# A hybrid decoder layer on one Trainium2 core: the order of small matmuls in attention and retention

## The chip, the cores and the metric

One NeuronCore of one Trainium2 chip runs the whole step. Its engines work side by side and wait for each other through semaphores: TensorE (PE in the profile; its weight loads are PEld), VectorE (DVE), ScalarE (ACT), GpSimd (POOL) and SyncE (SP), which here issues most DMAs. The metric is the device time of one execution in microseconds; the time before is the median of three runs.

## The reference, cut to what matters

One layer on 512 prompt tokens and 8 sequences of 4 sample tokens, all in float32: a combined projection, then eight heads of retention beside sixteen heads of sliding-window attention, an output projection, and a convolutional FFN. The two parts that the change touches are these:

```python
def retention_chunk(S, qkv):              # 4 chunks of 128 tokens; 8 heads, q and k 64 wide, v 128 wide
    q, k, v = qkv
    ...
    scores = jnp.einsum('bihd,bjhd->bhij', q, k) * dmask[None]
    o = jnp.einsum('bhij,bjhv->bihv', scores, v)
    o = o + jnp.einsum('bihd,bhdv->bihv', q, S) * jnp.exp((idx + 1.0)[:, None] * lg[None, :])[None, :, :, None]
    ...
def sink_attention(q, kk, vv, qpos, kpos, sinks):   # 16 query heads, 2 key heads, 64 wide; window of 128
    s = jnp.einsum('bnqkgd,bnskd->bnkgqs', q.astype(F32), kk.astype(F32)) * (SWA_DH ** -0.5)
    ...
    p = p / (jnp.sum(p, axis=-1, keepdims=True) + jnp.exp(sink - m))
    return jnp.einsum('bnkgqs,bnskd->bnqkgd', p, vv.astype(F32))
```

## The kernel before, in words

Most matmuls are float32 products made of three products of rounded halves (`mm3`: lines 174 and 178, 96 matmuls of 128x272 for one projection of 128 columns). Thirty-four such projections fill the first 604 us: per pair of retention heads one of q, one of k and two of v, then the attention's k and v, its eight q pairs and the eight gates. The output projection follows (to about 798 us), then the FFN, which takes the rest.

Retention and attention are cut into Python generators that are advanced between the projections' matmuls: `project` calls `slot_fast` after 32 and 64 of its 96 matmuls and `slot` after 48, and both again at its end. The generator `retention` is in the list `active` (advanced by `slot`), `swa_stream` and after it `swa_sample` in the list `fast`. So the small matmuls stand in PE's queue between those of the projections. The framework that records the program moves some instructions on each engine a little; PE then works its queue in order.

A head is 64 wide, and two heads share the 128 partitions: `half(0)` is partitions 0 to 63 and `half(1)` is 64 to 127. A product over one head therefore runs over 64 rows of PE's array (the profile writes 64\*128: 64 rows, 128 columns), where a projection runs over all 128 (128\*128). Four places mix the two kinds:

- `scores(i)` in `swa_stream`, 16 blocks of work (two heads of each key head, 128 queries each): for each key head `kv` and each `j`, a matmul over 128 rows with `kX[kv]` (line 721, the two cross products of the halves of q and k) and then one over 64 rows with `kH` (line 722) into the same place of the PSUM tile `sc`. VectorE then masks, scales and takes the maximum (line 725); `softmax` follows, and `turn` transposes the result on PE (line 700) for `outputs` (line 683).
- `scores(hh)` in `retention`, once for each half and each of four head pairs: four matmuls over 64 rows (line 494). Half 0 is issued one slot before half 1. Each float32 matmul of this kind is two passes in the profile, so 4 matmuls are 8 records.
- The outputs of a chunk in `retention` (lines 529 and 531): for each half, scores times v over 128 rows, then q times the state S over 64 rows. Chunk 0 has no state, so there are three chunks with both kinds for each of four head pairs: 12 places.
- The end of `swa_sample` (lines 809 and 810): for each of two key heads and eight sequences, a matmul over 128 rows that yields 64 output rows (128\*64) and one over 32 rows (32\*64).

PSUM is used through `small()`: a ring of four tiles with one name, each a bank of 128x512 float32.

Of the kernel before, what the change touches and what calls it, by code (L numbers as in the profile page):

```python
# [106 lines left out]
def trunk_kernel(  # L107
# [9 lines left out]
    pe, dve, act, pool = nc.tensor, nc.vector, nc.scalar, nc.gpsimd  # L117
# [3 lines left out]
    mult, add, sub = ALU.mult, ALU.add, ALU.subtract  # L121
# [77 lines left out]
    def small():  # L199
        return ps.tile([128, 512], F32, name="sm", tag="sm")  # L200
# [4 lines left out]
    def b4(shape, name, dtype=F32):  # L205
        return at.tile(shape, dtype, name=name, tag="b4", bufs=4)

    def g2(shape, name, dtype=F32):
        return at.tile(shape, dtype, name=name, tag="g2", bufs=4)

    def toks(c):
        return slice(128 * (c % 2), 128 * (c % 2) + 128)

    def half(i):
        return slice(64 * i, 64 * i + 64)

    def flat(a):
        return a.rearrange("p a b -> p (a b)")

    def halves_of(a):  # L220
        return a.rearrange("p (u c) -> p u c", u=2)
# [125 lines left out]
    band = late[:, 1128:1384]  # L347
# [21 lines left out]
    dmt = rtab[:, 0:1024].rearrange("p (h i) -> p h i", h=RH)  # L369
# [112 lines left out]
    def retention(p, q3, k2, v2):  # L482
# [5 lines left out]
            pool.tensor_copy(out=dst, in_=qd[half(hh), :, 256:272].rearrange("p u (b t) -> p u b t", t=4))  # L488
        sms = []

        def scores(hh):
            pss = small()
            for c in range(4):
                pe.matmul(pss[:, 128 * c:128 * c + 128], lhsT=kr[half(hh), c // 2, toks(c)], rhs=qr[half(hh), c // 2, toks(c)], start=True, stop=True)
            sm = g2([128, 4, 128], "smk")
            dve.tensor_tensor(out=sm, in0=pss.rearrange("p (c i) -> p c i", c=4),
                              in1=dmt[:, 2 * p + hh, :].unsqueeze(1).broadcast_to([128, 4, 128]), op=mult)
            sms.append(sm)

        yield  # L500
        pt, pts = to_tokens(kr, ksm)
# [1 line left out]
                          in1=kdt[:, 2 * p:2 * p + 2].unsqueeze(1).unsqueeze(3).broadcast_to([128, 4, 2, 64]), op=mult)  # L503
        for hh in range(2):
            dve.tensor_scalar(out=kd2[32 * hh:32 * hh + 32, half(hh)], in0=pts[:, half(hh)],
                              scalar1=kdst[:32, 2 * p + hh:2 * p + hh + 1], scalar2=None, op0=mult)
        scores(0)
        yield
        scores(1)
        for hh in range(2):  # L510
            pss = small()
            pe.matmul(pss[:32, 0:32], lhsT=ksm[half(hh), :], rhs=qsm[half(hh), :], start=True, stop=True)
            r = slice(32 * hh, 32 * hh + 32)
            dve.tensor_tensor(out=sm2[r, r], in0=pss[:32, 0:32], in1=dmst[:, 2 * p + hh, :], op=mult)
        S, ons, on = None, None, None
# [9 lines left out]
        for c in range(4):  # L525
            yield
            obs = [small(), small()]
            for hh in range(2):
                pe.matmul(obs[hh][:, 0:128], lhsT=sms[hh][:, c, :], rhs=vt[:, hh, c, :], start=True, stop=(S is None))
                if S is not None:  # L530
                    pe.matmul(obs[hh][:, 0:128], lhsT=qd[half(hh), c // 2, toks(c)], rhs=S[half(hh), :], start=False, stop=True)
            up = small()
            for hh in range(2):
                pe.matmul(up[half(hh), 0:128], lhsT=kd[:, c, half(hh)], rhs=vt[:, hh, c, :], start=True, stop=True)
            Sn = at.tile([128, 128], F32, name="S", tag="S", bufs=3)
            if S is None:
                dve.tensor_copy(out=Sn, in_=up[:, 0:128])
            else:
                dve.scalar_tensor_tensor(out=Sn, in0=S, scalar=gt[:, p:p + 1], in1=up[:, 0:128], op0=mult, op1=add)
            S = Sn  # L540
            if c == 0:
                ob = small()
                for b in range(NB):
                    pe.matmul(ob[:64, 0:128], lhsT=qm[:, 64 * b:64 * b + 64], rhs=Ss[:, b, :], start=(b == 0), stop=False)
                pe.matmul(ob[:64, 0:128], lhsT=sm2, rhs=v2, start=False, stop=True)
            if c == 1:
                pt = small()
                pe.transpose(out=pt[:, 0:64], in_=ons, identity=ident[:64, :64])
                for hh in range(2):
                    act.activation(out=C[:, 2 * p + hh, :, 256:272], in_=halves_of(pt[:, 32 * hh:32 * hh + 32]), func=AF.Copy,  # L550
                                   scale=gnw[:, 2 * p + hh:2 * p + hh + 1])
                for g in range(2):
                    up = small()
                    pe.matmul(up, lhsT=kd2, rhs=vm[:, 4 * g:4 * g + 4, :].rearrange("p b v -> p (b v)"), start=True, stop=True)
                    sl = Ss[:, 4 * g:4 * g + 4, :]
                    dve.scalar_tensor_tensor(out=sl, in0=sl, scalar=gt[:, 4 + p:5 + p], in1=up.rearrange("p (b v) -> p b v", b=4), op0=mult, op1=add)
                st(out=ret_s[0, :, 2 * p:2 * p + 2].rearrange("b h d v -> (h d) b v"), in_=Ss)
            if c == 2:
                back(on, 0)
            if c % 2 == 0:  # L560
                on = g2([128, 2, 2, 128], "on")
            norm_rows([o[:, 0:128] for o in obs], [on[:, c % 2, hh, :] for hh in range(2)])
            if c == 0:
                ons = at.tile([64, 128], F32, name="ons", tag="ons", bufs=1)
                norm_rows([ob[:64, 0:128]], [ons])
                vm = b4([64, NB, 128], "vm")
                dve.tensor_tensor(out=vm, in0=v2.unsqueeze(1).broadcast_to([64, NB, 128]), in1=bmask[:64, :].unsqueeze(2).broadcast_to([64, NB, 128]), op=mult)
# [5 lines left out]
    kH = at.tile([128, SEQ], F32R, name="kH")  # L573
    kX = [at.tile([128, SEQ], F32R, name=f"kX{i}") for i in range(2)]
    vS = at.tile([128, 4, 2, 128], F32R, name="vS")
    vsk = at.tile([32, 128], F32, name="vsk")
# [47 lines left out]
    scl, qSs = {}, {}  # L624
# [47 lines left out]
    def swa_stream():  # L672
# [34 lines left out]
        def scores(i):  # L707
            hp, n = i // 4, i % 4
            h0 = 2 * hp
            qS = qSs[hp, n // 2]  # L710
            k0 = max(0, 128 * (n - 1))
            w, off = (128, 128) if n == 0 else (256, 0)
            s = b4([128, 4, 256], "s")
            mx = at.tile([128, 4], F32, name="mx", tag="mx", bufs=3)
            den = at.tile([128, 4], F32, name="den", tag="den", bufs=3)
            for kv in range(2):
                sc = small()
                for j in range(2):
                    q_ = qS[:, j, kv, toks(n)]
                    o = sc[:, 256 * j:256 * j + 256]  # L720
                    pe.matmul(o, lhsT=q_, rhs=kX[kv][:, k0:k0 + 256], start=True, stop=False)  # L721
                    pe.matmul(o, lhsT=q_[half(kv)], rhs=kH[half(kv), k0:k0 + 256], start=False, stop=True)  # L722
                for j in range(2):
                    i_ = 2 * j + kv
                    dve.tensor_tensor_reduce(out=s[:, i_, 0:w], in0=sc[:, 256 * j:256 * j + w], in1=band[:, off:off + w], scale=scl[h0 + j][:, n, kv:kv + 1],
                                             scalar=-3.0e38, op0=add, op1=ALU.max, accum_out=mx[:, i_:i_ + 1])
            softmax(s, w, mx, flat(sinkb[:, h0:h0 + 2, :]), flat(nsinkb[:, h0:h0 + 2, :]), den)
            probs[i] = s, w
            if n == 0:
                split_q(hp, 1)  # L730
# [14 lines left out]
    def swa_sample():  # L745
        kc, vc = b4([128, NB, 128], "kc"), b4([128, NB, 128], "vc")
# [17 lines left out]
        for u in range(2):  # L764
            dve.tensor_tensor(out=qsa[:, 4 * u:4 * u + 4].rearrange("p b h t -> p h b t"),
                              in0=C[:, 8:16, u, 256:272].rearrange("p h (b t) -> p h b t", t=4),
                              in1=y[:, :, 16 * u:16 * u + 16].rearrange("p h (b t) -> p h b t", t=4), op=mult)
# [11 lines left out]
        for kv in range(2):  # L779
            r = half(kv)  # L780
            sc = small()
            scv = sc[:, 0:320].rearrange("p (g j) -> p g j", g=2)
            for b in range(NB):
                q_ = qsa[r, b, :, :].rearrange("p h t -> p (h t)")
                o = slice(32 * (b % 4), 32 * (b % 4) + 32)
                pe.matmul(scv[o, b // 4, 0:128], lhsT=q_, rhs=kcT[r, b, :], start=True, stop=True, tile_position=(64 * kv, 32 * (b % 4)))
                pe.matmul(scv[o, b // 4, 128:160], lhsT=q_, rhs=ksmp[r, :], start=True, stop=True, tile_position=(64 * kv, 32 * (b % 4)))
            for g in range(2):
                i = 2 * kv + g
# [9 lines left out]
        pTs = b4([128, 2, 512], "pTs")  # L799
# [2 lines left out]
        yield  # L802
        po = small()
        pov = po[:, 0:256].rearrange("p (b x) -> p b x", b=NB)
        for kv in range(2):
            r = half(kv)
            for b in range(NB):
                o = 128 * (2 * kv + b // 4) + 32 * (b % 4)
                pe.matmul(pov[r, b, :], lhsT=vc[:, b, r], rhs=pTs[:, 0, o:o + 32], start=True, stop=False)
                pe.matmul(pov[r, b, :], lhsT=vsk[:, r], rhs=pTs[:32, 1, o:o + 32], start=False, stop=True)  # L810
        for u in range(2):
            dve.tensor_copy(out=C[:, 8:16, u, 256:272].rearrange("p h (b t) -> p h b t", t=4),
                            in_=pov[:, 4 * u:4 * u + 4, :].rearrange("p b (h t) -> p h b t", t=4))
# [515 lines left out]
```

## Time and profile before

| What | Value |
| --- | --- |
| Runs | 2279.88, 2281.12, 2283.51 us; median 2281.12 |
| Profiled execution | 2281.43 us, span 2279.7 us |
| PE busy | 2215.3 us, 97% of the span, 17159 matmuls |
| DVE, ACT, POOL busy | 1632.7 us (72%), 1010.3 us (44%), 292.7 us (13%) |
| Chain that ended last | PE 66%, issue 17%, DVE 8%, DMA 5% |
| Mean granted clock of TensorE | 0.984 |

The span runs from the first to the last instruction; the execution's own time lies 1.7 us above it. Busy time counts overlapping records once, so a PE that is 97% busy may still hold small matmuls that run one by one. The chain is followed back from the last instruction, at each step to what released it.

### The profile page before, as it was taken

What the parts mean: (1) busy time and instruction counts of PE and PEld (TensorE: products, weight loads), DVE (VectorE), ACT (ScalarE), POOL (GpSimd) and SP (SyncE); (2) the same over time, 40 slices, a digit from 0 to 9 for tenths busy, and PEclk for the clock granted to TensorE, in tenths of its full rate; (3) what the DMA queues carried; (4) which work ended last, traced back from release to release, by engine and by line L of the source; (5) the groups of instructions that cost most, each with busy time, mean ns of one, the idle gap of its engine ahead of it and who ended that gap; (6) DMA issues with size and microseconds to landing.
All of it is one profiled execution on the core that took longest, in us unless ns stands there. A gap on an engine that the chain in (4) does not pass through costs nothing.

```text
span 2279.7 us, 42004 instructions
## 1 busy us (share of the span) xinstructions
PE 2215.3 (97%) x17159; PEld 2161.7 (95%) x17159; DVE 1632.7 (72%) x2457; ACT 1010.3 (44%) x1612; POOL 292.7 (13%) x463
## 2 busy tenths in 40 slices
PE   8999999999999979999999999999998999899998
PEld 7999999999999979999999999999998999898898
DVE  5545466766435788888888888888888766767775
ACT  5122234556413454444444444444446444445443
POOL 1000000000001312212112112112112101101000
PEclk8999999999999989999999999999999999999999
DMA  9333333213373343443444344344347556657553
GB/s 284 99 95 89 82 83 79 73 54 104 78 162 117 101 136 110 126 132 119 125 123 123 116 128 121 117 128 126 118 123 228 140 121 178 155 135 212 145 147 97
DMA packets 452656, 286.52 MB, mean 126 GB/s; under 512 B 46320, under 2 KB 430640, under 8 KB 452080
## 3 DMA queue, kind: packets, MB, share of 16 engines
q1 hardware_dynamic: 433376, 222.16, 35.7%
q0 software_dynamic: 19088, 61.68, 9.0%
q8 instruction: 134, 2.20, 0.4%
q14 instruction: 58, 0.48, 0.1%
HBM read 231.38 MB, written 47.67 MB: 122 GB/s over the span
## 4 chain that ended last, share of the span: by engine, by line
PE 66%; issue 17%; DVE 8%; DMA 5%; POOL 2%; ACT 1%; SPq 1%; DVEq 0%; POOLq 0%; ACTq 0%
PE acc L174 18%; PE acc L178 9%; PE bx L1090 6%; PE bx L1089 6%; PE bx L1092 6%; PE zy L1090 5%; PE zy L1089 5%; PE zy L1092 4%; DMA uraw<-in_w_up_dram 3%; DVE ulo L151 3%; POOL x_keep L1257 1%; DMA A_lo<-hx_keep 1%; PE sm L722 1%; PE sm L721 1%; DVE uraw L1132 1%
## 5 line engine op out<-in xcount | busy, mean ns | idle before, releaser
L151 DVE TENSOR_TENSOR ulo<-uraw,uhi 128x1024 fp32r<-128x1024 f32 (+1 forms) x272 | 321.9, 1187 | 87.9 <-ACT uhi L150 87.6
L150 ACT CAST uhi<-uraw 128x1024 fp32r<-128x1024 f32 (+1 forms) x272 | 278.1, 1023 | 110.0 <-issue 72.0
L150 ACT CAST uhi<-usum 128x1024 fp32r<-128x1024 f32 (+1 forms) x204 | 209.2, 1026 | 229.9 <-DVE usum L1125 124.8
L1090 PE MATMUL bx<-X_hi,ulo 128*128 128x272 f32 x1056 | 278.7, 295 | 13.0 <-DVE ulo L151 12.8
L1089 PE MATMUL bx<-X_lo,uhi 128*128 128x272 f32 x1056 | 277.4, 293 | 10.5 <-ACT uhi L150 10.4
L174 PE MATMUL acc<-A_lo,whi 128*128 128x272 f32 x1344 | 286.3, 294 | 1.2 <-ACT whi L150 0.6
L174 PE MATMUL acc<-A_hi,wlo 128*128 128x272 f32 x1344 | 281.1, 290 | 0.0
L1089 PE MATMUL bx<-A_lo,uhi 128*128 128x272 f32 x1056 | 271.8, 290 | 6.1 <-ACT tu L1127 2.7
L151 DVE TENSOR_TENSOR ulo<-usum,uhi 128x1024 fp32r<-128x1024 f32 (+1 forms) x204 | 242.4, 1188 | 47.1 <-ACT uhi L150 47.0
L1089 PE MATMUL zy<-A_lo,uhi 128*128 128x272 f32 x1056 | 272.7, 290 | 2.1 <-ACT p L1114 1.2
L1090 PE MATMUL zy<-A_hi,ulo 128*128 128x272 f32 x1056 | 271.6, 289 | 0.7 <-DVE ulo L151 0.7
L1090 PE MATMUL bx<-A_hi,ulo 128*128 128x272 f32 x1056 | 270.8, 288 | 0.0
L150 ACT CAST whi<-raw 128x1024 fp32r<-128x1024 f32 x100 | 104.8, 1048 | 293.3 <-PE acc L178 247.6
L1090 PEld LDWEIGHTS bx<-X_hi,ulo 128*128 128x128 f32 x1056 | 203.8, 193 | 17.3 <-DVE ulo L151 17.1
L174 PEld LDWEIGHTS acc<-A_lo,whi 128*128 128x128 f32 x1344 | 212.0, 190 | 7.7 <-issue 4.2
L1089 PEld LDWEIGHTS bx<-X_lo,uhi 128*128 128x128 f32 x1056 | 203.2, 192 | 12.2 <-ACT uhi L150 11.6
L174 PEld LDWEIGHTS acc<-A_hi,wlo 128*128 128x128 f32 x1344 | 212.2, 189 | 1.2
L1089 PEld LDWEIGHTS bx<-A_lo,uhi 128*128 128x128 f32 x1056 | 199.7, 189 | 7.4 <-ACT tu L1127 3.3
L1089 PEld LDWEIGHTS zy<-A_lo,uhi 128*128 128x128 f32 x1056 | 199.7, 189 | 3.2 <-ACT p L1114 1.8
L1090 PEld LDWEIGHTS zy<-A_hi,ulo 128*128 128x128 f32 x1056 | 199.7, 189 | 0.9 <-DVE ulo L151 0.9
L1090 PEld LDWEIGHTS bx<-A_hi,ulo 128*128 128x128 f32 x1056 | 199.5, 189 | 0.0
L178 PE MATMUL acc<-A_hi,whi 128*128 128x272 f32 x1344 | 189.0, 292 | 0.0
(437 smaller groups left out, 4315.5 us busy)
## 6 DMA issues: line engine op xcount, KB each, us to landing
uraw<-in_w_up_dram SPq DMA_DIRECT2D x176, 512.0 KB
uraw<-in_w_down_dram SPq DMA_DIRECT2D x64, 448.0 KB
raw<-in_w_in_dram SPq DMA_DIRECT2D x52, 512.0 KB
uraw<-in_w_down_dram SPq DMA_DIRECT2D x32, 512.0 KB
hx_keep<-us POOLq DMA_DIRECT2D x88, 136.0 KB, 2.0
hx_keep<-tt POOLq DMA_DIRECT2D x66, 136.0 KB, 4.7
x_keep<-us POOLq DMA_DIRECT2D x32, 272.0 KB, 5.2
raw<-in_w_in_dram SPq DMA_DIRECT2D x32, 256.0 KB
```

Source lines behind the costliest of these rows:

```text
L150: act.copy(out=hi, in_=src)
L151: eng.tensor_tensor(out=lo, in0=src, in1=hi.bitcast(F32), op=sub)
L174: pe.matmul(acc[:, u, :HC], lhsT=w, rhs=x[:, u, :], start=(first and i == 0 and w is wh), stop=False)
L178: pe.matmul(acc[:, u, :HC], lhsT=wh, rhs=xh[:, u, :], start=False, stop=(last and i == n - 1))
L721: pe.matmul(o, lhsT=q_, rhs=kX[kv][:, k0:k0 + 256], start=True, stop=False)
L722: pe.matmul(o, lhsT=q_[half(kv)], rhs=kH[half(kv), k0:k0 + 256], start=False, stop=True)
L1089: pe.matmul(bank, lhsT=hi[:, k], rhs=xl[:, k], start=(first and k == 0), stop=False, skip_group_check=True)
L1090: pe.matmul(bank, lhsT=lo[:, k], rhs=xh[:, k], start=False, stop=False, skip_group_check=True)
L1092: pe.matmul(bank, lhsT=hi[:, k], rhs=xh[:, k], start=False, stop=(k == n - 1), skip_group_check=True)
L1132: dve.tensor_tensor(out=a21, in0=a21, in1=a11, op=add)
L1257: sth(out=x1_keep[2 * mp + i], in_=y[:, i], accum_op=add)
```

## The change

At each of the four places the matmuls over 128 rows are now issued together, and then those over fewer rows, with the two halves (or the two key heads) in turn. In `swa_stream` and in retention's `scores` both halves' PSUM tiles are taken at the start, and VectorE's work on both follows all the matmuls; in retention both halves now stand in the later of the two slots. No matmul is added or removed, and operands and PSUM places stay the same. Where several products now share a bank, the first alone has `start=True`.

```diff
-        def scores(hh):
-            pss = small()
+        def scores():
+            pss = [small(), small()]
             for c in range(4):
-                pe.matmul(pss[:, 128 * c:128 * c + 128], lhsT=kr[half(hh), c // 2, toks(c)], rhs=qr[half(hh), c // 2, toks(c)], start=True, stop=True)
...
+                for hh in range(2):
+                    pe.matmul(pss[hh][:, 128 * c:128 * c + 128], lhsT=kr[half(hh), c // 2, toks(c)], rhs=qr[half(hh), c // 2, toks(c)],
+                              start=True, stop=True)
...
-        scores(0)
         yield
-        scores(1)
+        scores()
...
             for hh in range(2):
                 pe.matmul(obs[hh][:, 0:128], lhsT=sms[hh][:, c, :], rhs=vt[:, hh, c, :], start=True, stop=(S is None))
-                if S is not None:
+            if S is not None:
+                for hh in range(2):
                     pe.matmul(obs[hh][:, 0:128], lhsT=qd[half(hh), c // 2, toks(c)], rhs=S[half(hh), :], start=False, stop=True)
...
+            scs = [small(), small()]
+            for first in (True, False):
+                for j in range(2):
+                    for kv in range(2):
+                        q_ = qS[:, j, kv, toks(n)]
+                        o = scs[kv][:, 256 * j:256 * j + 256]
+                        if first:
+                            pe.matmul(o, lhsT=q_, rhs=kX[kv][:, k0:k0 + 256], start=(j == 0), stop=False, skip_group_check=True)
+                        else:
+                            pe.matmul(o, lhsT=q_[half(kv)], rhs=kH[half(kv), k0:k0 + 256], start=False, stop=True, skip_group_check=True)
...
-        for kv in range(2):
-            r = half(kv)
+        for first in (True, False):
             for b in range(NB):
...
+                for kv in range(2):
+                    r = half(kv)
+                    o = 128 * (2 * kv + b // 4) + 32 * (b % 4)
+                    if first:
+                        pe.matmul(pov[r, b, :], lhsT=vc[:, b, r], rhs=pTs[:, 0, o:o + 32], start=(b == 0), stop=False, skip_group_check=True)
+                    else:
+                        pe.matmul(pov[r, b, :], lhsT=vsk[:, r], rhs=pTs[:32, 1, o:o + 32], start=False, stop=True, skip_group_check=True)
```

Lines 721 and 722 become 726 and 728; 494 becomes 495; 529, 531 and 534 become 531, 534 and 537; 809 and 810 become 818 and 820.

PE, the third block of `scores` in `swa_stream`, before (kX0 and kX1 are the 128-row operands of the two key heads, kH the 64-row one; sm with two numbers are the two PSUM tiles):

```order
L721 MATMUL sm_4092<-kX0_497,qS_3868 128x256
L700 MATMUL sm_4071<-early_73,s_3919 128x128 x3
L700 MATMUL sm_4080<-early_73,s_3919 128x128 x3
L722 MATMUL sm_4092<-kH_496,qS_3868 128x256
L721 MATMUL sm_4092<-kX0_497,qS_3868 128x256
L722 MATMUL sm_4092<-kH_496,qS_3868 128x256
L721 MATMUL sm_4099<-kX1_498,qS_3868 128x256
L722 MATMUL sm_4099<-kH_496,qS_3868 128x256
L721 MATMUL sm_4099<-kX1_498,qS_3868 128x256
L722 MATMUL sm_4099<-kH_496,qS_3868 128x256
```

The same block now:

```order
L726 MATMUL sm_4092<-kX0_497,qS_3868 128x256
L703 MATMUL sm_4071<-early_73,s_3919 128x128 x3
L703 MATMUL sm_4080<-early_73,s_3919 128x128 x3
L726 MATMUL sm_4093<-kX1_498,qS_3868 128x256
L726 MATMUL sm_4092<-kX0_497,qS_3868 128x256
L726 MATMUL sm_4093<-kX1_498,qS_3868 128x256
L728 MATMUL sm_4092<-kH_496,qS_3868 128x256
L728 MATMUL sm_4093<-kH_496,qS_3868 128x256
L728 MATMUL sm_4092<-kH_496,qS_3868 128x256
L728 MATMUL sm_4093<-kH_496,qS_3868 128x256
```

The row count changed four times each way (eight changes with the one after the block) and now changes once each way. Nine of the 16 blocks stand like this. In six the recorder still puts the two key heads apart, as in the first block now:

```order
L178 MATMUL acc_3748<-A_hi_78,whi_3595 128x272 x2
L726 MATMUL sm_3839<-kX0_497,qS_3815 128x256 x2
L728 MATMUL sm_3839<-kH_496,qS_3815 128x256 x2
L178 MATMUL acc_3748<-A_hi_78,whi_3595 128x272
L726 MATMUL sm_3840<-kX1_498,qS_3815 128x256 x2
L728 MATMUL sm_3840<-kH_496,qS_3815 128x256 x2
L178 MATMUL acc_3748<-A_hi_78,whi_3595 128x272 x13
```

There the row count changes four times, and the halves do not alternate. The remaining block changes four times too, and has one pair of halves in turn.

PE, the outputs of chunk 1 of the first head pair in `retention`, before (smk are the masked scores, S the state):

```order
L178 MATMUL acc<-A_hi,whi 128x272 x16
L529 MATMUL sm<-C,smk 128x128
L531 MATMUL sm<-S,qd 128x128
L529 MATMUL sm<-C,smk 128x128
L531 MATMUL sm<-S,qd 128x128
L534 MATMUL sm<-C 64x128 x2
```

And now:

```order
L178 MATMUL acc<-A_hi,whi 128x272 x16
L531 MATMUL sm<-C,smk 128x128 x2
L534 MATMUL sm<-S,qd 128x128 x2
L537 MATMUL sm<-C 64x128 x2
L551 MATMUL sm<-early,ons 128x64
```

Two of the four changes of the row count are gone, in each of the 12 places. Retention's scores stood in two groups of four (line 494, four changes of the row count for each head pair) and stand in one of eight (line 495, two changes); lines 809 and 810 changed 31 times among themselves and beside the projection, and now stand as 16 and 16. The orders of ACT, POOL and SP are the same as before, line for line; DVE's differ where its work on these scores stands a few rows later.

## Rows read from the trace of the kernel before

**Rows 1.** Busy time by stretch: retention's, then the attention's.

```profile
core 0: us, PE busy (x) PEld busy (x) DVE busy (x) ACT busy (x) POOL busy (x), PEclk, DMA share, GB/s
60.00:340.00 280.00, 280.00 (x2133) 261.58 (x2132) 149.75 (x379) 61.37 (x119) 2.63 (x8) 1.00 0.33 88
340.00:560.00 220.00, 219.85 (x1589) 202.45 (x1588) 150.20 (x451) 121.93 (x303) 0.00 (x0) 1.00 0.32 80
```

**Rows 2.** Timeline of PE, a block of attention scores and later outputs.

```profile
start us, us, engine line op out<-in xcount [idle before <-releaser]
389.81 0.38 PE L721 MATMUL sm<-kX,qS 128*128 128x256 f32 x1
...
391.68 2.15 PE L178 MATMUL acc<-A_hi,whi 128*128 128x272 f32 x15
...
396.80 0.39 PE L683 MATMUL sm<-pl,vS 128*128 128x256 f32 x2
...
397.74 0.41 PE L174 MATMUL acc<-A_lo,whi 128*128 128x272 f32 x2
```

**Rows 3.** Timeline of PE, retention's outputs of chunk 1.

```profile
116.40 0.49 PE L529 MATMUL sm<-C,smk 128*128 128x128 f32 x2
116.82 0.49 PE L531 MATMUL sm<-S,qd 64*128 64x128 f32 x2
117.23 0.44 PE L534 MATMUL sm<-C 128*64 128x128 f32 x4
```

**Rows 4.** Timeline of PE, retention's scores of half 1, then of the samples.

```profile
99.12 1.16 PE L494 MATMUL sm<-qr,kr 64*128 64x128 f32 x8
100.20 0.25 PE L512 MATMUL sm<-smp 64*32 64x32 f32 x4
```

**Rows 5.** Timeline of all engines, the first matmuls of the samples' outputs.

```profile
585.26 0.30 PE L809 MATMUL sm<-pTs,vc 128*64 128x32 f32 x2
585.49 0.30 PE L810 MATMUL sm<-pTs,vsk 32*64 32x32 f32 x2
```

**Rows 6.** Groups of PE's instructions, 580 to 600 us.

```profile
L809 PE MATMUL sm<-pTs,vc 128*64 128x32 f32 x32 | 5.2, 246 | 0.0
```

**Rows 7.** Timeline of PE, retention's outputs of chunk 0 and the state's update.

```profile
106.53 0.61 PE L529 MATMUL sm<-C,smk 128*128 128x128 f32 x4
107.07 0.44 PE L534 MATMUL sm<-C 128*64 128x128 f32 x4
```

**Rows 8.** Busy time by stretch around 591 us.

```profile
589.00:590.00 1.00, 1.00 (x10) 0.84 (x10) 0.00 (x0) 0.00 (x0) 0.00 (x0) 1.00 0.31 100
...
591.00:592.00 1.00, 1.00 (x8) 0.85 (x6) 0.00 (x0) 0.00 (x0) 0.00 (x0) 0.50 0.00 0
```

**Rows 9.** Chain that ended last, 585 to 604 us (start, us, what).

```profile
591.06 0.35 PE sm L810 x2
...
593.51 3.92 PE acc L178 x16
...
601.68 2.01 PE acc L178 x16
```

**Rows 10.** Busy time by stretch, two later waits of PE.

```profile
1748.00:1751.00 3.00, 0.81 (x7) 0.59 (x5) 3.00 (x4) 3.00 (x4) 0.85 (x1) 1.00 1.03 356
1751.00:1752.00 1.00, 0.83 (x5) 0.83 (x6) 1.00 (x2) 1.00 (x2) 0.00 (x0) 0.74 1.05 336
...
1767.00:1771.00 4.00, 0.70 (x6) 0.65 (x6) 4.00 (x6) 2.29 (x4) 0.00 (x0) 1.00 0.01 2
```

**Rows 11.** Timeline of DVE, the first mask on the scores of that block.

```profile
391.10 0.48 DVE L725 CUSTOM_DVE_ANT_0 s<-sm,late,qy 128x256 f32<-128x256 f32 x1
```

**Rows 12.** Timeline of ACT, up to the exponentials of that block.

```profile
397.93 0.37 ACT L688 COPY pl__4341<-sm 64x256 f32<-64x256 f32 x1 [2.85 <-PE sm L683]
...
398.73 0.51 ACT L664 ACTIVATE s<-s,nm 128x256 f32<-128x256 f32 x1
```

**Rows 13.** Timeline of all engines, retention's mask on the scores of half 1.

```profile
100.31 0.69 DVE L496 TENSOR_TENSOR smk<-sm,C 128x512 f32<-128x512 f32 x1 [0.36 <-PE sm L494]
```

More of the change, by code (lines that the diff above doesn't have):

```diff
@@ L489, in retention @@
         sms = []
-        def scores(hh):
-            pss = small()
+        def scores():
+            pss = [small(), small()]
             for c in range(4):
-                pe.matmul(pss[:, 128 * c:128 * c + 128], lhsT=kr[half(hh), c // 2, toks(c)], rhs=qr[half(hh), c // 2, toks(c)], start=True, stop=True)
[L495 to L498, printed above, removed]
+                for hh in range(2):
+                    pe.matmul(pss[hh][:, 128 * c:128 * c + 128], lhsT=kr[half(hh), c // 2, toks(c)], rhs=qr[half(hh), c // 2, toks(c)],
+                              start=True, stop=True)
+            for hh in range(2):
+                sm = g2([128, 4, 128], "smk")
+                dve.tensor_tensor(out=sm, in0=pss[hh].rearrange("p (c i) -> p c i", c=4),
+                                  in1=dmt[:, 2 * p + hh, :].unsqueeze(1).broadcast_to([128, 4, 128]), op=mult)
+                sms.append(sm)
         yield
@@ L529, in retention @@
                 pe.matmul(obs[hh][:, 0:128], lhsT=sms[hh][:, c, :], rhs=vt[:, hh, c, :], start=True, stop=(S is None))
-                if S is not None:
+            if S is not None:
+                for hh in range(2):
                     pe.matmul(obs[hh][:, 0:128], lhsT=qd[half(hh), c // 2, toks(c)], rhs=S[half(hh), :], start=False, stop=True)
@@ L715, in scores @@
             den = at.tile([128, 4], F32, name="den", tag="den", bufs=3)
-            for kv in range(2):
[L717 to L722, printed above, removed]
+            scs = [small(), small()]
[8 more added lines that the diff above has]
+                            pe.matmul(o, lhsT=q_[half(kv)], rhs=kH[half(kv), k0:k0 + 256], start=False, stop=True, skip_group_check=True)
+            for kv in range(2):
                 for j in range(2):
                     i_ = 2 * j + kv
-                    dve.tensor_tensor_reduce(out=s[:, i_, 0:w], in0=sc[:, 256 * j:256 * j + w], in1=band[:, off:off + w], scale=scl[h0 + j][:, n, kv:kv + 1],
+                    dve.tensor_tensor_reduce(out=s[:, i_, 0:w], in0=scs[kv][:, 256 * j:256 * j + w], in1=band[:, off:off + w], scale=scl[h0 + j][:, n, kv:kv + 1],
                                              scalar=-3.0e38, op0=add, op1=ALU.max, accum_out=mx[:, i_:i_ + 1])
@@ L804, in swa_sample @@
         pov = po[:, 0:256].rearrange("p (b x) -> p b x", b=NB)
-        for kv in range(2):
-            r = half(kv)
+        for first in (True, False):
             for b in range(NB):
-                o = 128 * (2 * kv + b // 4) + 32 * (b % 4)
-                pe.matmul(pov[r, b, :], lhsT=vc[:, b, r], rhs=pTs[:, 0, o:o + 32], start=True, stop=False)
-                pe.matmul(pov[r, b, :], lhsT=vsk[:, r], rhs=pTs[:32, 1, o:o + 32], start=False, stop=True)
+                for kv in range(2):
[5 more added lines that the diff above has]
+                        pe.matmul(pov[r, b, :], lhsT=vsk[:, r], rhs=pTs[:32, 1, o:o + 32], start=False, stop=True, skip_group_check=True)
         for u in range(2):
```

## The prediction, made before the result was known

> **What bounds the kernel now.** I read the page first: PE is busy for 97% of the span, so the question is whether its time in the changed places is work or only occupancy. The windows by stretch come next. From 60 to 340 us, where retention runs between the projections, PE is busy 280.00 of 280 us; from 340 to 560 us, where the attention runs, 219.85 of 220, while DVE has 150.20 and ACT 121.93 [rows 1]. Nothing else sets the end there: what PE no longer needs comes off the time, until another engine is late. After 604 us nothing in the program changes, so that part only moves forward.
>
> The timeline of PE then shows what a change of the row count costs. In a block of attention scores, matmuls over 128 and over 64 rows alternate. From the L721 at 389.81 to the L178 at 391.68 there are six, so each takes 1.87 / 6 = 0.312 us. The eight L683 from 396.80 to 397.74 have the same 256 columns and other weights each time, and all run over 128 rows: 0.94 / 8 = 0.1175 us each [rows 2]. A change of the row count costs the difference, 0.194 us.
>
> Retention's passes of 128 columns give the same. Two with a change at either end take 0.42 us (L529 at 116.40, L531 at 116.82) [rows 3]; eight with a change at either end take 1.08 us (L494 at 99.12 to L512 at 100.20) [rows 4]. Six more passes are 0.66 us, so a pass is 0.11 us and a change 0.20 us. In the samples' outputs a group of two passes takes 0.23 us (585.26 to 585.49) [rows 5]; the second ends 0.30 - 0.246 = 0.054 us after the first [rows 5, 6], so a change there costs 0.23 - 0.115 = 0.115 us, taking a pass as 0.0575.
>
> **The change, part by part.** It removes no matmul; it removes changes of the row count, and it lets halves overlap. I count the first in the order of instructions.
>
> Changes removed:
> - Attention scores: nine blocks go from 8 changes to 2, seven from 8 to 4 (the six that still stand apart by key head and the mixed one): 54 + 28 = 82, at 0.194: 15.9 us.
> - Retention's outputs: 12 places lose two each: 24 at 0.20: 4.8 us.
> - Retention's scores: four head pairs go from two groups to one: 8 at 0.20: 1.6 us.
> - Samples' outputs: 31 become 1: 30 at 0.115: 3.4 us.
>
> Sum 25.7 us.
>
> Halves in turn: no row shows two matmuls of 64 rows and 128 columns in alternating halves, so this is bounded. Four passes over alternating row halves, but with 32 columns of weights, span only 0.25 us (L512), where L494 in one half needs 0.11 us for each pass [rows 4]. Four passes over two column halves (L534) span 0.44 us, and four in one place (L529) 0.61 [rows 7]; that is about two pitches less, though L534 also pays for a change. So the second of a pair is nearly free there. At the other end it saves nothing. I take nearly free, since both nearest rows show it, at 0.10 us saved: 32 second passes of L495 (3.2 us), 24 of L534 (2.4 us), 19 of L728 at 0.11 (2.1 us), and 32 of L818 and L820 at 0.05 (1.6 us). Sum 9.3 us, bounds 0 and 9.3.
>
> The clock: during the samples' outputs, which are thin work for 8.2 us, the granted clock falls from 1.00 at 589 us to 0.50 at 591 [rows 8], from 2.4 to 1.2 GHz. Seven groups of two then take 0.35 us, not 0.23 [rows 5, 9], and the next 16 L178 take 3.92 us, where 16 at full clock take 2.01 [rows 9]: 0.8 + 1.9 = 2.7 us lost. The block will last 8.2 - 0.8 - 3.4 - 1.6 = 2.4 us. Other stretches of about that length go both ways: PE idle for most of 1748 to 1751 us loses the clock right after, and idle for most of 1767 to 1771 it keeps it [rows 10]. Bounds 0 and 2.7; I take the middle, 1.4 us.
>
> What is late next: VectorE's masks on the first key head now wait for all eight matmuls. Before, the first mask began at 391.10, 0.58 us before the block ended [rows 2, 11]; now it cannot begin until about the end. Behind it in DVE's queue stand the other masks, and the softmax waits for them, and PE's transposes for that. But the exponentials of this block began at 398.73, behind an ACT copy that had waited 2.85 us for PE's L683 at 397.9 [rows 12]: six microseconds in which half a microsecond disappears. PE's own distance from the end of the block to those L683 stays the same. Retention's half 0 scores come one slot later; their mask (0.69 us, as at 100.31 for half 1) [rows 13] can follow the other by about 101.7, and the first reader is the L529 at 106.53 [rows 7]. The DMAs and ACT keep their order. New waits: below nothing is excluded, as nothing is issued earlier in the block but the second half's first matmul; above, 1.0 us (two masks of 0.48) for each of 16 blocks, if the mask chain always ended last. I take 1 us in all, near the lower end, for that block's slack.
>
> The profiled execution took 2281.4 us (its span is 2279.7), 0.3 above the median of the runs, so no correction is needed. 2281.4 - 25.7 - 9.3 - 1.4 + 1.0 = **2246.0 us**.
>
> **The rivals.**
> - The halves do not overlap when 128 columns of weights are loaded for each. The 32-column rows are then no guide, and only the changes count: 2246.0 + 9.3 = 2255. Against it: two kinds of tile overlap already [rows 4, 7]. For it: neither has this width in row halves.
> - Turning from one half to the other counts as a change itself. Then the overlap is lost and about 29 turns in the attention's blocks, 28 + 12 in retention's at 0.20 and 30 among the samples' at 0.115 are added, 5.6 + 8.0 + 3.4 = 17 us: 2255 + 17 = 2272. Against it: L512 and L534 turn within 0.25 and 0.44 us for four passes.
> - The masks come too late in most blocks, and PE waits at its transposes: 16 blocks at 1.0 us: 2246.0 - 1.0 + 16 = 2261. For it: DVE is busy 68% of that stretch [rows 1]; against it, the slack above.
> - Weight loads decide: the load for a matmul waits until an earlier one on the same rows is through. Then 128-row matmuls side by side gain nothing, the 25.7 us fall away and only the overlap is left: 2281.4 - 9.3 - 1.4 + 1.0 = 2272. The eight L683 speak against it: 0.1175 us apart with new weights each, while two of them span 0.39 [rows 2]. The Trainium skill states this mechanism (TensorE: Matmul & The Clock Gate, Part 3: Packing small matmuls — row/col tiling): a weight load overlaps running matmuls only where the row groups differ. The trace does not agree, by those same 0.1175 us.
> - Slower than before: the ring of four PSUM tiles. The second key head's tile is now needed by the second matmul of a block instead of the fifth. If its last reader stands in a queue behind a wait for PE, PE stops for as long as such a wait lasts, 2.85 us [rows 12], in each of 16 blocks: 45.6 us, 2246.0 + 45.6 = 2292. It decides from 35.4 / 16 = 2.2 us for a block. Against it: PE loses 0.15 of 220 us in that stretch today [rows 1], and the tile's last user is older than the block.
>
> **How the numbers follow.** My forecast gets 66 of 100, no overlap 16, late masks 8, turns as changes 4, weight loads 2, the PSUM ring 3, and 1 for savings that vanish altogether. Within my forecast the time lies between 2243 (clock kept, no wait) and 2249. The range goes to 2240, for a few microseconds of clock or waits gained elsewhere, and to 2261, which takes in no overlap and late masks. A change of 0.2% (4.6 us) is what a measurement can tell here; all cases but the last two are faster by more: 0.95 faster, 0.02 within, 0.03 slower.
>
> **What would show it.** In a whole block, four L726 and then four L728 in about 1.2 us up to the next L178, where there were 2.5; two L728 starting within 0.02 us of each other; eight L495 in some 1.1 us for 16 passes; L818 and L820 together about 2.4 us. The clock around them either stays at 1.00 or falls to 0.50. PE's idle time before L703 should stay under 2 us in total. I am wrong if two L728 start 0.1 us or more apart, if PE waits at L726 or L703, or if time after the output projection's start changes.

## The result and the profile after

The changed kernel takes 2244.93 us (median of 5 runs, 2239.99 to 2247.5) where the kernel before takes 2281.12 in the same comparison: a ratio of 0.9846, with a 95% interval from 0.9832 to 0.9861. The forecast was 2246.0.

The executions differ by some microseconds in parts that nothing changed, so the experiments are read by a stretch of PE's queue as well as by the whole time. It starts at the first L423, which stands ahead of all changed matmuls, and ends at the output projection's first matmul with B_lo, which stands behind them all. Timeline of PE, before, its two ends (the second is the row that starts at 603.53):

```profile
78.01 0.49 PE L423 MATMUL sm<-early,va 128*128 128x128 f32 x3
...
603.53 0.41 PE L174 MATMUL acc<-B_lo,whi 128*128 128x272 f32 x2
```

The same rows of the kernel after:

```profile
77.02 0.60 PE L423 MATMUL sm<-early,va 128*128 128x128 f32 x4
...
564.22 0.41 PE L174 MATMUL acc<-B_lo,whi 128*128 128x272 f32 x2
```

The stretch lasted 525.52 us and lasts 487.20: 38.3 us less. The two profiled executions are 41.4 apart (2281.43 and 2239.99); the other 3.1 lie where no matmul moved, 1.0 ahead of the stretch and the rest behind it. What lies behind took 1676.2 us (span 2279.7 less 603.53) and takes 1674.0; over all the kernels below it runs from 1669.8 to 1677.6, in no order that goes with their edits.

PE is still what bounds it. Page of after, busy time by engine:

```profile
PE 2176.6 (97%) x17159; PEld 2139.1 (96%) x17159; DVE 1630.1 (73%) x2457; ACT 1010.7 (45%) x1612; POOL 291.9 (13%) x463
```

Windows of after, retention's stretch and the attention's (columns as in [rows 1]):

```profile
60.00:330.00 270.00, 270.00 (x2153) 255.55 (x2153) 148.93 (x382) 62.98 (x123) 1.66 (x8) 1.00 0.36 94
330.00:540.00 210.00, 209.85 (x1651) 202.84 (x1650) 153.47 (x454) 127.29 (x306) 0.00 (x0) 1.00 0.34 85
```

The busy share says nothing of the gain: it was 100% of these stretches before and is again, because a PE that runs small matmuls one by one counts as busy. What shows it is the distance between matmuls. Timeline of PE, a whole block of attention scores in after:

```profile
371.55 0.37 PE L726 MATMUL sm<-kX,qS 128*128 128x256 f32 x1
...
372.50 0.59 PE L726 MATMUL sm<-kX,qS 128*128 128x256 f32 x3
373.02 0.50 PE L728 MATMUL sm<-kH,qS 64*128 64x256 f32 x4
373.46 0.52 PE L178 MATMUL acc<-A_hi,whi 128*128 128x272 f32 x2
```

Seven matmuls stand between 372.50 and 373.46: 0.96 us, where six took 1.87 [rows 2]. The four L728 take 0.44 us up to the next L178, one change of the row count and two pairs; in the single records the second of a pair starts 3 to 4 ns after the first.

Timeline of PE, retention's scores in after, then the samples' scores:

```profile
96.85 1.16 PE L495 MATMUL sm<-qr,kr 64*128 64x128 f32 x16
97.94 0.25 PE L514 MATMUL sm<-smp 64*32 64x32 f32 x4
```

Sixteen passes take 1.09 us, where eight took 1.08 [rows 4]. Retention's outputs of a chunk with a state, in the same view:

```profile
113.41 0.61 PE L531 MATMUL sm<-C,smk 128*128 128x128 f32 x4
113.95 0.49 PE L534 MATMUL sm<-S,qd 64*128 64x128 f32 x4
114.37 0.44 PE L537 MATMUL sm<-C 128*64 128x128 f32 x4
```

Four L534 passes take 0.42 us, where two L531 took 0.41 [rows 3].

The samples' outputs, in the chain that ended last (start, us, what):

```profile
554.03 1.06 PE sm L818 x32
555.08 1.05 PE sm L820 x32
556.13 0.46 PE acc L178 x2
```

8.25 us (585.26 to 593.51, [rows 5, 9]) became 2.10, and the L178 behind them stay at full speed. Windows of after there:

```profile
554.00:555.00 1.00, 1.00 (x33) 0.97 (x32) 0.00 (x0) 0.00 (x0) 0.00 (x0) 1.00 0.92 257
...
557.00:558.00 1.00, 1.00 (x10) 1.00 (x9) 0.70 (x2) 1.00 (x3) 0.00 (x0) 1.00 0.72 232
```

The granted clock stays at 1.00 where it fell to 0.50 [rows 8].

No wait came in. Groups of PE's instructions in after (60 to 800 us), where the last number is the idle time before them:

```profile
L703 PE MATMUL sm<-early,s 128*128 128x128 f32 x112 | 17.2, 274 | 0.2
L726 PE MATMUL sm<-kX,qS 128*128 128x256 f32 x64 | 14.2, 310 | 0.0
...
L728 PE MATMUL sm<-kH,qS 64*128 64x256 f32 x64 | 11.4, 331 | 0.0
```

To see what each place gave, I added up, over its matmuls, the distance from the end of the matmul before to its own end:

| Place | before | after | gain | forecast |
| --- | --- | --- | --- | --- |
| attention scores (64 + 64 matmuls) | 35.9 | 17.8 | 18.1 | 15.9 + 2.1 |
| retention's outputs | 19.4 | 12.2 | 7.2 | 4.8 + 2.4 |
| retention's scores, with the matmul behind them | 10.5 | 4.9 | 5.6 | 1.6 + 3.2 |
| samples' outputs, with the matmul behind them | 8.7 | 2.4 | 6.3 | 3.4 + 1.6 + 0.8 (clock) |
| the 16 L178 after that matmul (clock) | 3.6 | 2.0 | 1.6 | 1.9 (clock) |

Of the clock's 0.8 and 1.9 the forecast took 1.4, about half. The gains come to 38.8 us, 0.5 more than the stretch lost: behind retention's scores eight matmuls are counted before and four after, at about 0.125 us each.

### The profile page after: what moved, and what is told of

It is laid out like the page before. It is cut to its first block, busy times and chain, and to the rows that moved or that the text cites. A ratio compares the mean times of both kernels' runs of the same rounds, so it can differ in the third digit from the quotient of the medians.

```text
span 2238.2 us, 42004 instructions
## 1 busy us (share of the span) xinstructions
PE 2176.6 (97%) x17159; PEld 2139.1 (96%) x17159; DVE 1630.1 (73%) x2457; ACT 1010.7 (45%) x1612; POOL 291.9 (13%) x463
## 4 chain that ended last, share of the span: by engine, by line
PE 64%; issue 18%; DVE 9%; DMA 6%; POOL 2%; ACT 1%; SPq 1%; DVEq 0%; POOLq 0%; ACTq 0%
PE acc L174 17%; PE acc L178 9%; PE bx L1100 7%; PE bx L1099 6%; PE bx L1102 6%; PE zy L1099 5%; PE zy L1100 5%; PE zy L1102 4%; DMA uraw<-in_w_up_dram 3%; DVE ulo L151 3%; DMA A_lo<-hx_keep 1%; POOL x_keep L1267 1%; DVE cv L1186 1%; DVE us L1191 1%; PE sm L686 1%
## 5 line engine op out<-in xcount | busy, mean ns | idle before, releaser
L178 PE MATMUL acc<-A_hi,whi 128*128 128x272 f32 x1344 | 187.6, 290 | 0.0
```

Source lines behind the costliest of these rows:

```text
L178: pe.matmul(acc[:, u, :HC], lhsT=wh, rhs=xh[:, u, :], start=False, stop=(last and i == n - 1))
```

## The experiments

All were run beside the kernel before. "Stretch" is the one above, from each run's single profile; before it is 525.52 us. The start-up ahead of it varies by itself (from the first L386 to the first L423, 23.1 to 26.1 us), which is why I start it there.

| Kernel | median us | ratio to before [95%] | stretch us | against before |
| --- | --- | --- | --- | --- |
| scores_only | 2257.22 | 0.9912 [0.9893, 0.9932] | 508.88 | -16.6 |
| retention_only | 2264.23 | 0.9948 [0.9930, 0.9966] | 513.09 | -12.4 |
| samples_only | 2265.68 | 0.9959 [0.9942, 0.9977] | 517.50 | -8.0 |
| samples_in_two | 2273.28 | 0.9988 [0.9976, 0.9999] | 524.42 | -1.1 |
| after_again | 2236.24 | 0.9830 [0.9814, 0.9846] | 487.17 | -38.4 |
| no_turn | 2240.40 | 0.9849 [0.9830, 0.9869] | 492.22 | -33.3 |
| padded | 2230.22 | 0.9804 [0.9784, 0.9825] | 481.34 | -44.2 |
| padded_state_first | 2231.85 | 0.9800 [0.9780, 0.9820] | 480.57 | -45.0 |
| padded_old_order | 2233.37 | 0.9824 [0.9803, 0.9846] | 480.88 | -44.6 |

The first four ran together (before: 2276.13), the next four together (2275.65), the last alone (2274.11). The expected times below are counted from the first comparison, where the kernel before took 2281 us, and so lie 5 to 7 us high; that is why after_again's 2236.24 us lies under the 2240 to 2248 expected for it. The ratios and the stretches can be compared.

**One part at a time.** The first three take over one hunk of the change each: that of `swa_stream`, those of `retention`, that of `swa_sample`.

scores_only:

> The kernel before, with the attention's scores alone regrouped. If a change of the row count costs 0.194 us (82 of them go) and the second of a pair of halves in turn is nearly free (19 pairs), 15.9 + 2.1 = 18.0 us come off: about 2263 us, and the clock still falls in the samples' outputs. If halves in turn did not overlap: 2265. If the gain of the whole change came from elsewhere (the clock, earlier results): 2279 to 2281.

retention_only:

> The kernel before, with retention's scores and outputs alone regrouped. 32 changes at 0.20 us and 56 second passes of a pair at 0.10 us: 6.4 + 5.6 = 12.0 us, about 2269 us. If halves in turn did not overlap: 2275. If the later slot of the first half's scores makes VectorE's mask late, PE waits at the outputs over the masked scores and part of the 12 us is missing.

samples_only:

> The kernel before, with the samples' outputs alone regrouped. 30 changes at 0.115 us and 32 second passes at 0.05 us: 5.0 us; with the clock kept at full speed after them 2.7 us more: 7.7 us, about 2273.4 us. If the clock falls all the same: 2276.1.

The parts give 16.6, 12.4 and 8.0 us, 37.1 together, where the whole gives 38.3. Each lies near its own sum (18.0, 12.0, 7.7), and the 1.4 that the attention's part lacks is the clock: its scores alone gave 18.1 by place, as in the whole change. That kernel still has the thin 8.9 us of the samples' outputs. Its windows there:

```profile
562.00:563.00 1.00, 1.00 (x9) 0.81 (x10) 0.00 (x0) 0.00 (x0) 0.00 (x0) 0.85 0.14 51
563.00:564.00 1.00, 1.00 (x7) 0.81 (x7) 0.00 (x0) 0.00 (x0) 0.00 (x0) 0.50 0.02 6
```

The clock fell at 562.70 and came back at 572.94, 10.2 us, where before it was away for 6.8 (590.96 to 597.78): 3.4 us more at half speed. So in this profile one part's gain was partly eaten in another's place. With the samples' outputs alone put in order, the chain reads:

```profile
585.36 1.06 PE sm L811 x32
586.41 1.05 PE sm L813 x32
587.46 2.21 PE acc L178 x16
```

Sixteen L178 take 2.21 us behind it and not 3.92 [rows 9]: clock kept, 8.0 us gained, of which the sum put 2.7 down to the clock.

**The clock alone.** samples_in_two keeps the old order and its 31 changes, but lets the projection's matmuls in between the two key heads:

```diff
             for b in range(NB):
...
                 pe.matmul(pov[r, b, :], lhsT=vsk[:, r], rhs=pTs[:32, 1, o:o + 32], start=False, stop=True)
+            if kv == 0:
+                yield
```

> The kernel before, with the samples' outputs of the second key head issued one slot later, so that 4 us of projection matmuls stand between two thin stretches of 4 us each; no matmul changes its kind or neighbours otherwise. If the length of the thin stretch makes the clock fall, it stays at 1.00 here and the time is 2281.1 - 2.7 = 2278.4 us (up to 0.5 us of that lost to a later split of the attention's output). If the clock falls whatever stands between, 2281 or a little above.

Chain of that kernel, what follows each of the two pieces of 3.7 us:

```profile
586.90 2.21 PE acc L178 x16
...
594.78 3.46 PE acc L174 x16
```

The first piece kept the clock, the second lost it (0.50 from 595.31 to 598.73, half as long as before). 1.1 us gained, near half of the 2.7. The fall thus goes with the thin work ahead of it, and cutting that work in two without removing a change gave part of the price back. The two pieces, of one length, went both ways; what decided between them stays open. By the medians this kernel gained 2.9 us (95% interval 0.2 to 5.5), and one profile does not tell how often the second piece keeps the clock.

**Whether the halves must stand in turn.** no_turn is the changed kernel with three pairs of loops exchanged, so that within the 64- and 32-row matmuls one half comes first and then the other:

```diff
-            for c in range(4):
-                for hh in range(2):
+            for hh in range(2):
+                for c in range(4):
...
-                for j in range(2):
-                    for kv in range(2):
+                for kv in range(2):
+                    for j in range(2):
```

and the same for `b` and `kv` in `swa_sample`. after_again is the changed kernel, run beside it.

> The changed kernel again, as the measure for the three beside it: 2240 to 2248 us.

> The changed kernel with the halves one after the other instead of in turn, in the attention's scores, retention's scores and the samples' outputs; the grouping by row count stays, and with it the 46 changes at the scores. (Retention's outputs hold one matmul of each half and cannot be taken apart.) If the overlap of halves is worth what was forecast, 2.1 + 3.2 + 1.6 = 6.9 us come back: about 2252 us. If only the changes of the row count matter: the time of the changed kernel. If a turn from half to half costs like a change: faster than the changed kernel by up to 14 us.

It lost 5.0 us of the stretch (4.2 by the medians, 2240.40 against 2236.24); about 1.4 of that is the clock, which fell again behind its samples' outputs (below: 16 L178 in 3.61 us, against the 2.21 at full clock), so the turn is worth 3.6 us by the stretch; by place it is 3.7: 2.2 for L495, nothing for L728 and 1.5 for L818 and L820. The turn also alternates the PSUM tiles, but in after so do the L726 over 128 rows, and those end 0.116 to 0.119 us apart: alternating the tiles alone makes no pairs. The 6.9 that I expected for it was wrong for L728 altogether and for L495 by 1.0. Timeline of PE in no_turn, retention's scores, then a block of the attention's:

```profile
93.74 1.71 PE L495 MATMUL sm<-qr,kr 64*128 64x128 f32 x16
95.38 0.25 PE L514 MATMUL sm<-smp 64*32 64x32 f32 x4
...
362.88 0.50 PE L728 MATMUL sm<-kH,qS 64*128 64x256 f32 x4
363.31 0.90 PE L178 MATMUL acc<-A_hi,whi 128*128 128x272 f32 x5
```

Sixteen L495 passes take 1.64 us where the turn made it 1.09, but the four L728 take 0.43 as before. Their single records start 7 and 5 ns apart in pairs, although the program has two of one half and then two of the other. The signal that belongs to the last of the first half's two is carried by the third record, so one of the other half started ahead of it. Among the sixteen L495 passes the signal of the eighth is carried by the eleventh record: three of the other half started early, and only there do ends lie 4 to 5 ns apart; elsewhere 107 to 112 ns. The Trainium skill (TensorE: Matmul & The Clock Gate, Part 3: Packing small matmuls — row/col tiling) holds that matmuls start and end in program order; these records do not agree.

Chain of no_turn at the samples' outputs:

```profile
553.02 1.77 PE sm L818 x32
554.80 1.85 PE sm L820 x32
556.65 3.61 PE acc L178 x16
```

3.62 us of thin work instead of 2.10, without a change of the row count inside, and the clock fell at 556.34.

**Whether the row count is the price.** If a change costs 0.194 us, it should pay to have none: padded gives the 64-row operand a zeroed other half, so that all score matmuls run over 128 rows. To make room for the second tile, three small tiles share others' storage and S has two buffers instead of three.

```diff
-    kH = at.tile([128, SEQ], F32R, name="kH")
+    kZ = [at.tile([128, SEQ], F32R, name=f"kZ{i}") for i in range(2)]
+    for i in range(2):
+        pool.memset(kZ[i][half(1 - i)].bitcast(F32), 0.0)
...
-                            pe.matmul(o, lhsT=q_[half(kv)], rhs=kH[half(kv), k0:k0 + 256], start=False, stop=True, skip_group_check=True)
+                            pe.matmul(o, lhsT=q_, rhs=kZ[kv][:, k0:k0 + 256], start=False, stop=True, skip_group_check=True)
```

> The changed kernel with the attention's 64-row matmuls turned into 128-row ones: kH is held in two tiles whose other half is zero, so the product is the same and no row count changes in the scores. (To make room, four small tiles share memory with others.) The remaining 46 changes at 0.194 us go, 8.9 us; the 19 overlapped matmuls each cost a full 0.1175 us again, 2.1 us; a copy of 64 rows is added once. About 6.5 us faster than the changed kernel: 2238.5 us. If a matmul over 64 rows is itself cheaper or the changes were not the cost: the same as the changed kernel or slower.

Its stretch is 5.9 us shorter than after's, near the 6.5 expected: two changes gone in each of 23 groups (8.9), the pairs' overlap given up (2.1), and a copy added. Timeline of PE in padded, a whole block:

```profile
401.94 0.72 PE L729 MATMUL sm<-kX,qS 128*128 128x256 f32 x4
402.50 0.64 PE L731 MATMUL sm<-kZ,qS 128*128 128x256 f32 x4
402.97 0.67 PE L178 MATMUL acc<-A_hi,whi 128*128 128x272 f32 x4
```

The four L731 stand 0.47 / 4 = 0.118 us apart, and the L178 behind them follows at the same pace: neither end of the group costs anything. The 0.6 us lacking from the 6.5 lies in the other product: by place the L729 add up to 8.60 us, the L726 in after to 7.98. A few L729 come late; one ends 0.45 us after the matmul before it, where after's needs 0.12. So short waits did come in here; what ended them is not shown.

padded_state_first also moves the state's update matmuls (lines 534 and 537 here), so that one more change falls away where they stand beside the outputs:

```diff
-            if S is not None:
-                for hh in range(2):
-                    pe.matmul(obs[hh][:, 0:128], lhsT=qd[half(hh), c // 2, toks(c)], rhs=S[half(hh), :], start=False, stop=True)
...
+            if S is not None:
+                for hh in range(2):
+                    pe.matmul(obs[hh][:, 0:128], lhsT=qd[half(hh), c // 2, toks(c)], rhs=S[half(hh), :], start=False, stop=True)
```

> The padded kernel, with retention's state update (128 rows to 64 columns) issued between the outputs' 128-row and 64-row matmuls, so that in chunk 1 the 64-row ones stand beside the 64-row transposes: four changes of the row count fewer at 0.20 us, 0.8 us. About 2237.7 us, hardly to be told from the padded one by the time; its trace should show 0.8 us less from 52 to 330 us. If VectorE then reads the outputs later than it needs to, it is the same or slower.

The stretch is 0.8 us shorter than padded's; in the runs it cannot be told from it. That is one profile each, so it agrees and proves little.

padded_old_order is the control: all score matmuls over 128 rows, but kX and kZ alternating as in the kernel before.

```diff
-            for first in (True, False):
+            for kv in range(2):
                 for j in range(2):
-                    for kv in range(2):
+                    for first in (True, False):
```

> The padded kernel with the attention's scores issued in the order of the kernel before: for each key head and each j the matmul with kX, then the one with kZ, so the operands alternate as they did, but all run over 128 rows. If it is the change of the row count that costs, the alternating order is free: the time of the padded kernel, about 0.980 of the kernel before, and 8 x 0.118 us for a block. If what cost was the order itself (two operands in turn into one place of PSUM), the block takes 2.5 us again and the time is that of the changed kernel or worse, 0.983 to 0.990.

Timeline of PE in padded_old_order, four of a block's eight:

```profile
398.39 0.28 PE L731 MATMUL sm<-kZ,qS 128*128 128x256 f32 x1
398.51 0.28 PE L729 MATMUL sm<-kX,qS 128*128 128x256 f32 x1
398.63 0.28 PE L731 MATMUL sm<-kZ,qS 128*128 128x256 f32 x1
398.75 0.28 PE L729 MATMUL sm<-kX,qS 128*128 128x256 f32 x1
```

They stand 0.12 us apart, where the same order with 64-row matmuls stood 0.312 apart [rows 2], and the stretch is 480.88 us against padded's 481.34. (By the medians it gained 40.7 us on its kernel before and padded 45.4, with intervals of the ratio that overlap; the finding rests on the distances and the stretch.) So alternating the operands, or the two products, costs nothing; the row count is the price. The Trainium skill (TensorEngine Tiling (Array Packing), Key Properties) says that a change of the tiling mode drains TensorE, without a price. The price of 0.194 us for each change fits that; what PE does in this time the runs do not show.

## Why the prediction was right

- **PE's time in the changed places was occupancy, not work.** Right: what PE no longer needed there came off the time, and nothing behind the output projection's start moved beyond what it does by itself.
- **The changes of the row count, 0.194 and 0.20 us.** Right, and shown from both sides: the attention's part gave 18.1 us by place against 18.0, retention's outputs 7.2 against 7.2; and with no change of rows the old order runs at full pace (padded_old_order). Each group that remains still pays about 0.31 us for its first 64-row matmul and 0.32 for the first projection matmul behind it.
- **Halves nearly free in pairs.** Right in size: L495 does twice the passes in the same time, the L728 of a pair start 3 to 4 ns apart. The rivals of no overlap and of a turn that costs a change are out by that, and their 2255 and 2272 us lie above every run. What I took for a condition, that the halves stand in turn, holds for long groups only: four L728 pair up by themselves.
- **The clock.** Taken as 1.4 us, the middle of 0 and 2.7; it was kept in full, in this kernel and in the five other profiles whose samples' outputs lasted 2.1 us. This is one of the two terms that were mis-sized, by 1.3 us. Two readings of the samples' rows were loose. The 3.92 us of L178 include the change of the row count at their start, which the 2.01 lack; with it, 16 take 2.21 at full clock. And the 0.246 us of [rows 6] is a mean over both clocks: at full clock the second pass ends 0.059 us after the first, so a change there costs 0.109 and not 0.115. Neither moves the sum by more than 0.2 us.
- **New waits.** Taken as 1.0 us; there were none (0.2 us before L703 in all). The late masks and the PSUM ring are out: PE loses 0.15 us from 330 to 540 us, the same 0.15 as before. The ring's price was one wait of 2.85 us per block; none came.
- **Weight loads decide.** Out: three more L726 side by side, with other weights each, end 0.119 and 0.116 us apart.

The forecast for the stretch was 25.7 + 9.3 + 1.4 - 1.0 = 35.4 us, and 38.3 came off. Clock and waits make 2.3 of the 2.9 between them; the other 0.6 is about what retention's scores and the samples' outputs gave above their terms (0.3 and 0.5 by place, with retention's four matmuls taken off). That the whole time, 2244.93 us, came within 1.1 us of the forecast is luck in part: the median moved by 36.2 here and by 39.4 in the second comparison (2275.65 to 2236.24), because the part outside the stretch varies.

## What to carry to other kernels

Where a bound engine is 100% busy, measure the distance between its instructions, not its busy share: small matmuls over 64 rows between those over 128 cost 0.2 us for each change, more than the matmuls themselves. Put equal row counts together and the two halves in turn; where a change remains for a few matmuls only, filling the missing rows with zeros is cheaper still (another 5.9 us of the stretch here, and 2230.22 against 2236.24 us beside it, the fastest version of this study together with its two variants). A part's gain can be eaten in another's place by the clock, so thin stretches are worth shortening even where their own time is small.

## What the runs showed of the hardware

- PE does not always start matmuls in the program's order, as the description of the kernel before has it: in no_turn, among L495 passes the other half's were up to three ahead, which gave pairs although the program has none.
- Work that keeps PE "busy" at 1.00 can still lose the clock: 32-column matmuls over 8.2 to 8.9 us lost it in three kernels of three (before, scores_only, retention_only), over 3.6 to 3.7 us in two pieces of three, and over 2.1 us in none of six.
- The clock goes with the length of the start-up too: in two profiles (scores_only and padded_old_order) it stayed at 1.00 from about 20 us on through the start-up, in the nine others it fell to 0.50 once more, for 6.8 us between 47 and 59 us, and the time from the first L386 to the first L423 was 23.1 us in those two against 25.0 to 26.1. Windows of padded_old_order:

```profile
50.00:55.00 5.00, 5.00 (x40) 4.83 (x40) 1.81 (x5) 1.04 (x1) 0.00 (x0) 1.00 0.53 127
```

and of padded:

```profile
50.00:55.00 5.00, 5.00 (x25) 4.79 (x24) 1.19 (x4) 0.24 (x1) 0.00 (x0) 0.57 0.65 156
```

No edit touches that part, and why these two kept the clock is not shown. A comparison from the start of PE's work would have put 2.8 us down to an order that is worth none.
